# Moving the w_down sums to GpSimd's transfer queue, and placing weight rows and kept results two products earlier, in a one-core decoder layer

## Chip, core and metric

One core of a Trainium2 chip runs the whole layer as one launch. The metric is device time in microseconds, the median of several runs. The engines are named as the profile names them: PE (TensorE matmul) with its weight loads PEld, DVE (VectorE), ACT (ScalarE), POOL (GpSimd) and SP (SyncE). In this kernel SP computes nothing: it starts nearly all transfers, one after the other, and when one of them has to wait for a buffer or a result, all that stand behind it in SP's queue wait too.

## What is computed

The reference is one decoder layer on 2048 tokens of width 1024: sliding-window attention beside a convolution group, an output projection with a residual, and a SwiGLU feed-forward part with a residual. The change concerns the last of these alone:

```
hn = rms_norm(h, ffn_pre_g)
ff = (jax.nn.silu(hn @ w_gate) * (hn @ w_up)) @ w_down
h = h + rms_norm(ff, ffn_post_g)
```

D_MODEL is 1024, D_FF is 2816, and everything is float32.

## The kernel before

**Products.** A float32 matmul is made of three matmuls on 128 x 512 operands, from a rounded part and a remainder (`hl`, `w` and other tags hold the two side by side). ACT makes the rounded part of a weight (`split_f`, L824) and DVE the remainder (`lo`, L828). One *product* here is four 128-row blocks times three, that is 12 matmuls into one PSUM bank (`product`, L908).

**Feed-forward part.** The 2048 tokens are taken as two sets: tiles 0 and 1 first, then tiles 2 and 3. For each set the gate and up matrices (22 items: 11 pairs of blocks, gate and up in turn) go through the seven-product form of a 2 x 2 block multiplication. First `stage_pre` (L916) makes two of the block products for most items and stores the first of them in `keeps`. Then `stage_p1` (L992), the seven-product part, does the rest: five products for an item whose first product is kept (20 of 22 items in the first set), seven for the others, 114 products in the first set. Last, `stage_p2` (L1150) multiplies by w_down, again in seven-product form; it reads the results of p1 from `mids` and four sums of w_down blocks from `td`.

**Inside p1.** For item m, `loads(m)` (L1001) brings the two weight rows: `raw` (L1006) and `chl` (L1008), 512 KB each. `sums(m)` (L1011) has DVE make four weight sums S1 to S4 in further `chl` buffers. `fetch(m)` (L1034) brings the kept product into a `gb` buffer; ACT copies it into a PSUM bank (L1066) before the item's first product, so that the matmuls add to it. Each step first splits the weight operand of the product three steps ahead (`AHEAD = 3`), then issues its own product. Results leave through `y5` (L1076, a `gb` buffer) and `x2` (L1079, an `at` buffer), DVE adds, ACT's silu, and stores to `mids` (L1094, L1100, L1103). The pools have two buffers each for `gb`, `at` and `raw`, five for `chl`, four for `fa`, one pair for `wx` and three for `fc`.

**The w_down sums.** `stage_tsums` (L1112) runs beside the first set's p1. For each of 11 pairs it loads four w_down blocks of 256 KB (L1119: two into `wx`, two into `fc`), makes four differences on DVE in place, and stores each to `td` (L1125). One pair of `wx` buffers means that a pair's first load must wait until the previous pair's stores have landed. Beside this, DVE runs convolution taps of a later stage (tile `fc@C`).

**What sets the order.** The stages are generators. A `Lane` (L1307) hands out steps of a side stage in proportion to a cost that the main stage yields; the sums have the lane `lt` with rate `RT` (L1362), and each step's yield is its price. Code order gives priorities only. The framework then orders each engine's instructions by a simulated timeline, so a step that is ready early can be moved far ahead of its place in the code, and each engine and queue then executes its list strictly in order.

Of the kernel before, what the change touches and what calls it, by code (L numbers as in the profile page):

```python
# [26 lines left out]
T = 512  # L27
# [10 lines left out]
def layer_kernel(ctx, tc, x, xT, cols, rows, sinks, relb, onehot, w_in, w_pw, w_out, w_gate, w_up, w_down, out):  # L38
    nc = tc.nc
# [15 lines left out]
    def t_(tag, shape, dt=F32):  # L55
        return sb.tile(list(shape), dt, tag=tag, name=nm(tag), bufs=BUFS[tag])

    def f4(tag, shape=(P, D)):
        return t_(tag, shape)

    def f2(tag, shape=(P, T)):
        return t_(tag, shape)

    def hl(tag):
        return t_(tag, (P, 2, T), F32R)
# [757 lines left out]
    def split_f(x, w):  # L823
        act(w[:, 0], x, AF.Copy)  # L824
        return w

    def lo(x, w, on_pool):
        (ptt if on_pool else vtt)(w[:, 1], x, w[:, 0].bitcast(F32), ALU.subtract)  # L828
# [79 lines left out]
    def product(o, w, op, first):  # L908
        n = 0
        for k in range(4):  # L910
            ks = slice(k * P, (k + 1) * P)
            for a, b in ((0, 0), (0, 1), (1, 0)):
                mat(o, w[:, a, ks], op[k][:, b], start=first and n == 0, stop=n == 11, skip_group_check=not first)
                n += 1
# [77 lines left out]
    def stage_p1(ws, ops, mid, keep):  # L992
        PRE = PRES[ws[0]]
        L = f"F{ws[0]}"
        raws = {}
        todo = []
        for m in range(len(MATS)):
            st = [1, 2, 4, 5, 6] if m < PRE else list(range(7))
            todo += [(m, j, i, len(st)) for j, i in enumerate(st)]

        def loads(m):  # L1001
            if m < len(MATS):
                lab[0] = L
                src, pr = MATS[m]
                r0 = t_("raw", (P, 2, T))
                nc.sync.dma_start(r0, src[2 * pr].rearrange("p (a b) -> p a b", a=2))  # L1006
                r1 = t_("chl", (P, 2, T))
                nc.sync.dma_start(r1, src[2 * pr + 1].rearrange("p (a b) -> p a b", a=2))  # L1008
                raws[m] = dict(A11=r0[:, 0], A12=r0[:, 1], A21=r1[:, 0], A22=r1[:, 1])

        def sums(m):  # L1011
            if m < len(MATS):
                lab[0] = L
                r = raws[m]
                s12 = t_("chl", (P, 2, T))
                r["S1"], r["S2"] = s12[:, 0], s12[:, 1]
                vtt(r["S1"], r["A21"], r["A22"], ALU.add)
                vtt(r["S2"], r["S1"], r["A11"], ALU.subtract)
                s34 = t_("chl", (P, 2, T))
                r["S3"], r["S4"] = s34[:, 0], s34[:, 1]  # L1020
                vtt(r["S3"], r["A11"], r["A21"], ALU.subtract)
                vtt(r["S4"], r["A12"], r["S2"], ALU.subtract)

        wops = {}
        kept = {}

        def split(q):
            if q < len(todo):
                m, j, i, n = todo[q]
                lab[0] = L  # L1030
                wops[q] = split_f(raws[m][STEPS[i][1]], hl("w"))
                lo(raws[m][STEPS[i][1]], wops[q], ws[0] and i in POOL_LO)

        def fetch(m):  # L1034
            if m < PRE:
                lab[0] = L
                kept[m] = f2("gb")
                nc.sync.dma_start(kept[m], keep[m])

        loads(0)  # L1040
        sums(0)
        for q in range(AHEAD):
            split(q)
        loads(1)
        fetch(0)
        sg = {}
        for q, (m, j, i, nst) in enumerate(todo):
            pre = m < PRE
            gate = MATS[m][0] is w_gate
            pr = MATS[m][1]  # L1050
            split(q + AHEAD)
            lab[0] = L
            which, an, bn = STEPS[i]
            if len(ops.get(bn, ())) < 4:
                lh.until(f"S{ws[0]}")
                lab[0] = L
            if j == 0:
                bk = {}
                if not gate:
                    blocks = {}  # L1060
                    if pre:
                        blocks[3] = f2("fa")
                        nc.sync.dma_start(blocks[3], mid[0, pr])
                if pre:
                    bk["B"] = mm()
                    act(bk["B"], kept.pop(m), AF.Copy)  # L1066
            first = which not in bk
            if first:
                bk[which] = mm()
            o = bk[which]  # L1070
            product(o, wops.pop(q), ops[bn], first)
            if i == 0:
                bk["B"] = mm()
                act(bk["B"], o, AF.Copy)
            elif i == 1:
                y5 = f2("gb")  # L1076
                act(y5, o, AF.Copy)
            elif i == 2:
                x2 = f2("at")  # L1079
                act(x2, o, AF.Copy)  # L1080
            else:
                v = {4: y5, 5: x2}.get(i, o)
                if v is not o:
                    vtt(v, v, o, ALU.add)
                if gate:
                    s = f2("fa")
                    act(s, v, AF.Silu)
                    sg[i] = s
                else:
                    s = sg.pop(i)  # L1090
                    vtt(s, s, v, ALU.mult)
                    blocks[i] = s
                    if i in (3, 4, 6):
                        nc.sync.dma_start(mid[{3: 0, 4: 4, 6: 1}[i], pr], s)  # L1094
                    if i == 5:
                        a11, a22, a21 = blocks[3], blocks[4], s
                        for to, o_, p_, op, q_ in ((5, a22, a21, ALU.add, a22), (3, a21, a11, ALU.subtract, a21),
                                                   (2, a11, a22, ALU.subtract, a11)):
                            (ptt if ws[0] else vtt)(o_, p_, q_, op)
                            nc.sync.dma_start(mid[to, pr], o_)  # L1100
                    if i == 6:
                        (ptt if ws[0] else vtt)(s, s, blocks[3], ALU.subtract)
                        nc.sync.dma_start(mid[6, pr], s)  # L1103
            if j == nst - 4:
                sums(m + 1)
            if j == nst - 2:
                fetch(m + 1)
            if j == nst - 1:
                loads(m + 2)
            yield 2.76  # L1110

    def stage_tsums(td):  # L1112
        L = "G0"
        for pr in range(NF // 2):
            lab[0] = L
            wx = f4("wx", (P, 2, T))
            b = [wx[:, 0], wx[:, 1], f2("fc"), f2("fc")]
            for i, (f, n) in enumerate(((0, 0), (0, 1), (1, 0), (1, 1))):
                nc.sync.dma_start(b[i], w_down[2 * pr + f, :, n * T : (n + 1) * T])  # L1119
            yield 3  # L1120
            b11, b12, b21, b22 = b
            for to, o, p_, q_ in ((0, b11, b12, b11), (2, b12, b22, b12), (1, b22, b22, b11), (3, b21, b21, b22)):
                lab[0] = L
                vtt(o, p_, q_, ALU.subtract)
                nc.sync.dma_start(td[to, pr], o)  # L1125
                yield 1

    def finish(L, gb, jobs, pool=True):
        lab[0] = L
# [229 lines left out]
    YL, YL2 = 12, 20  # L1359
    YZ = 1.0  # L1360
    W_LEAD = 4.0
    RT = 0.3  # L1362
    RP = 0.1
    NS = 12
    TIE = 5
# [10 lines left out]
    lh = Lane(1.2, 0)  # L1376
    lt = Lane(RT, 0)
    lu = Lane(0.6, 0)
# [67 lines left out]
    td = dr.tile([4, NF // 2, P, T], F32, name="td")  # L1446
# [7 lines left out]
    lh.add("S0", stage_h_sums(ws, ops), lambda: f"P0.{PRE_S0}" in started and "B3" in lb.done)  # L1454
    run(stage_pre(ws, ops, mids[0], keeps[0], Q0))
    lt.add("TS", stage_tsums(td))
    run(stage_p1(ws, ops, mids[0], keeps[0]))
    lt.until("TS")
    lc.until("T2")
# [11 lines left out]
    run(stage_pre(ws, ops, mids[1], keeps[1]))  # L1471
    lf.until("E0.3")
    run(stage_p1(ws, ops, mids[1], keeps[1]))
    run(stage_p2(ws, mids[1], td, True))

# [62 lines left out]
```

## Time and profile before

| what | value |
|---|---|
| median of 3 runs | 1996.32 us (1993.41 to 1996.72) |
| the profiled execution's own time | 1994.08 us |
| its span, first to last instruction | 1992.1 us |
| mean granted TensorE clock | 0.987 |
| busy: PE, DVE, ACT, POOL | 97%, 74%, 48%, 12% of the span |
| first set's p1, by its matmuls | about 682 us to 1021 us of the span |

PE is busy nearly all of the span, so the gaps that remain lie in few places, and averages over the span hide them. Tables by stretch of the span show them: busy time of each engine, instructions that began there (x), the granted clock, and the share of the 16 DMA engines. Tables of waits tell which event ended an idle stretch; a table for SP tells what held its queue. In names, `chl@F` is a buffer of tag `chl` in stage F (gate and up), `@G` is the w_down part with its sums, `@C` the convolution, and `a<-b` is written from read. L94 is the helper that issues every DVE arithmetic instruction and L85 the one of every matmul, so groups there are told apart by tile names.

### The profile page before, as it was taken

The numbers are of one execution on the slowest core, as the hardware profiler recorded it, in microseconds if no ns is written. First come the engines' busy times: TensorE is split into PE (matmuls) and PEld (weight loads), VectorE is DVE, ScalarE is ACT, GpSimd is POOL, SyncE is SP. The second block draws the span as 40 slices with busy tenths as digits, with TensorE's granted clock in tenths as the row PEclk, the third lists the DMA queues.
The fourth block names the chain that finished last, engine by engine and source line by source line (L and its number), as shares of the span: only waits on it lengthen the run. The fifth ranks groups of instructions, "written<-read, shape, count | busy, mean of one in ns | idle before, by whom it ended". The sixth has DMA issues, their size and how long they took to land.

```text
span 1992.1 us, 26622 instructions
## 1 busy us (share of the span) xinstructions
PE 1936.4 (97%) x8730; PEld 1550.4 (78%) x8730; DVE 1467.2 (74%) x2648; ACT 953.5 (48%) x1878; POOL 247.2 (12%) x339
## 2 busy tenths in 40 slices
PE   8999999999998999899999999998899999999997
PEld 6877777777776878678888788886788888888886
DVE  4999969995875899777659964667766765455557
ACT  5455354447546533234355464656543433345443
POOL 4011111101121000000000110000023332311003
PEclk9999999999999999999999999999999999999999
DMA  8786657566659767865478787759845542466664
GB/s 307 252 305 218 210 187 257 182 214 216 225 199 322 258 222 254 280 231 190 143 238 273 255 270 243 253 201 376 289 147 170 169 159 85 142 227 197 211 195 143
DMA packets 224810, 444.06 MB, mean 223 GB/s; under 512 B 22136, under 2 KB 47904, under 8 KB 224672
## 3 DMA queue, kind: packets, MB, share of 16 engines
q1 hardware_dynamic: 212768, 429.79, 64.8%
q10 hardware_dynamic: 11904, 12.59, 1.8%
q8 instruction: 68, 1.11, 0.2%
q14 instruction: 70, 0.57, 0.1%
HBM read 327.46 MB, written 114.83 MB: 222 GB/s over the span
## 4 chain that ended last, share of the span: by engine, by line
PE 77%; DMA 11%; DVE 6%; issue 2%; ACT 2%; POOL 1%; SPq 1%; DVEq 0%; POOLq 0%; ACTq 0%
PE mm@F L85 29%; PE mm@G L85 18%; PE mm@A L85 14%; PE mm@W L85 5%; PE tr@B L85 4%; PE tr@W L85 3%; DMA gb@F<-keeps 1%; DMA chl@F<-w_gate 1%; DMA raw@F<-w_gate 1%; PE mm@U L85 1%; DMA chl@G<-h_scr 1%; DVE fc@C L94 1%; DVE w@F L94 1%; DMA td<-fc@G 1%; PE tr@B L492 1%
## 5 line engine op out<-in xcount | busy, mean ns | idle before, releaser
L94 DVE SCALAR_TENSOR_TENSOR fc@C<-glu@C,colt,fc@C 128x512 f32<-128x512 f32 x480 | 357.1, 758 | 2.8
L85 PE MATMUL mm@F<-hl@H,w@F 128*128 128x512 f32 x1056 | 256.8, 394 | 8.1 <-ACT mm@F L954 8.1
L85 PEld LDWEIGHTS mm@F<-hl@H,w@F 128*128 128x128 f32 x1056 | 200.4, 190 | 51.5 <-ACT mm@F L954 9.5
L85 PE MATMUL mm@G<-hl@G,hl@G 128*128 128x512 f32 x924 | 228.0, 392 | 1.8 <-DVE hl@G L94 1.6
L85 PE MATMUL mm@A<-hl@A,w@A 128*128 128x512 f32 x840 | 209.4, 397 | 4.4 <-ACT w@A L127 1.8
L85 PEld LDWEIGHTS mm@G<-hl@G,hl@G 128*128 128x128 f32 x924 | 171.7, 188 | 38.9 <-DVE hl@G L94 2.4
L824 ACT ACTIVATE w@F<-chl@F 128x512 fp32r<-128x512 f32 x220 | 134.8, 624 | 138.9 <-PE mm@F L85 131.4
L85 PE MATMUL mm@G<-w@G,hl@G 128*128 128x512 f32 x876 | 199.4, 389 | 0.0
L85 PEld LDWEIGHTS mm@G<-w@G,hl@G 128*128 128x128 f32 x876 | 164.4, 188 | 34.1
L85 PEld LDWEIGHTS mm@A<-hl@A,w@A 128*128 128x128 f32 x840 | 156.6, 189 | 43.1 <-issue 3.1
L94 DVE TENSOR_TENSOR w@F<-chl@F,w@F 128x512 fp32r<-128x512 f32 x198 | 145.6, 739 | 37.9 <-ACT w@F L824 37.3
L85 PE MATMUL mm@F<-mid@H,w@F 128*128 128x512 f32 x528 | 137.4, 408 | 12.5 <-ACT mm@F L954 10.6
L85 PE MATMUL mm@F<-ql@H,w@F 128*128 128x512 f32 x528 | 128.5, 391 | 6.8 <-ACT mm@F L1066 4.8
L85 PE MATMUL mm@F<-p@H,w@F 128*128 128x512 f32 x528 | 132.5, 397 | 0.0
L85 PEld LDWEIGHTS mm@F<-mid@H,w@F 128*128 128x128 f32 x528 | 103.7, 198 | 36.8 <-ACT mm@F L954 11.9
L85 PE MATMUL mm@F<-x@H,w@F 128*128 128x512 f32 x528 | 126.7, 391 | 0.0
L85 PEld LDWEIGHTS mm@F<-ql@H,w@F 128*128 128x128 f32 x528 | 98.9, 188 | 29.3 <-ACT mm@F L1066 6.2
L85 PEld LDWEIGHTS mm@F<-p@H,w@F 128*128 128x128 f32 x528 | 101.7, 193 | 21.8 <-ACT at@F L1080 0.2
L85 PEld LDWEIGHTS mm@F<-x@H,w@F 128*128 128x128 f32 x528 | 98.4, 188 | 21.1 <-issue 0.8
L127 ACT ACTIVATE w@A<-raw@A 128x512 fp32r<-128x512 f32 x110 | 67.5, 626 | 92.3 <-PE mm@A L85 63.5
L94 DVE TENSOR_TENSOR w@G<-raw@G,w@G 128x512 fp32r<-128x512 f32 x73 | 52.1, 714 | 68.8 <-ACT w@G L824 67.7
L495 POOL TENSOR_SCALAR_AFFINE_SELECT p@B<-p@B 128x512 f32<-128x512 f32 x62 | 52.9, 863 | 361.2 <-ACT p@B L493 359.8
(302 smaller groups left out, 3224.8 us busy)
## 6 DMA issues: line engine op xcount, KB each, us to landing
mids<-fa@F SPq DMA_DIRECT2D x154, 256.0 KB, 2.6
raw@A<-w_in SPq DMA_DIRECT2D x55, 512.0 KB, 4.5
w@A<-lo_in SPq DMA_DIRECT2D x84, 256.0 KB, 3.5
fc@G<-mids SPq DMA_DIRECT2D x77, 256.0 KB, 3.5
fa@G<-mids SPq DMA_DIRECT2D x75, 256.0 KB, 4.2
gb@F<-keeps SPq DMA_DIRECT2D x72, 256.0 KB, 4.5
w@W<-fold SPq DMA_DIRECT2D x32, 512.0 KB, 5.3
chl@F<-w_gate SPq DMA_DIRECT2D x22, 512.0 KB, 4.0
```

The lines of the kernel that those rows point to most:

```text
L85: r = nc.tensor.matmul(*args, **kw)
L94: r = op(*args, **kw)
L127: act(w[:, 0], raw, AF.Copy)
L492: nc.tensor.transpose(o[:, i * P : (i + 1) * P], pr[:, 4 * g + i], ident)
L495: nc.gpsimd.affine_select(out=pg[:, kb].rearrange("p (i q) -> p i q", q=P), in_=pg[:, 1].rearrange("p (i q) -> p i q", q=P), compare_op=AL ...
L824: act(w[:, 0], x, AF.Copy)
```

## The change

```diff
 (stage_p1)
             elif i == 1:
-                y5 = f2("gb")
+                y5 = f2("at")
...
             if j == nst - 4:
+                fetch(m + 1)
                 sums(m + 1)
-            if j == nst - 2:
-                fetch(m + 1)
-            if j == nst - 1:
+            if j == nst - 3:
                 loads(m + 2)
             yield 2.76
 (stage_tsums)
-                nc.sync.dma_start(b[i], w_down[2 * pr + f, :, n * T : (n + 1) * T])
-            yield 3
+                nc.gpsimd.dma_start(b[i], w_down[2 * pr + f, :, n * T : (n + 1) * T])
+            yield 2.5
...
                 vtt(o, p_, q_, ALU.subtract)
-                nc.sync.dma_start(td[to, pr], o)
-                yield 1
+                nc.gpsimd.dma_start(td[to, pr], o)
+                yield 0.6
...
-    RT = 0.3
+    RT = 0.2
```

It does five things. The kept product of the next item is fetched two products earlier. The weight rows of the item after next are loaded two products earlier. The result `y5` takes its buffer from `at` instead of `gb`, so that `gb` holds kept products alone. All 88 transfers of the w_down sums (44 loads, 44 stores) go from SP's queue to GpSimd's. A pair of the sums costs 4.9 in place of 7 and is paid at rate 0.2 in place of 0.3, so it takes 24.5 us of the main stage's count instead of 23.3 us. No arithmetic is added or removed, and no byte more or less is moved. The code lines after the edit stand one line higher (L1118 and L1124 for the sums' transfers).

SP's queue near the start of the first set's p1, before (rows `td<-` are stores of finished sums, `<-w_down` their loads, `gb<-keeps` a kept product, `raw` and `chl` weight rows, `mids` results):

```order
L1125 DMA td<-fc@G_1124_6655 128x512
L1119 DMA wx@G_1131_6712<-w_down 128x512
L1125 DMA td<-fc@G_1123_6654 128x512
L986 DMA mids_4716<-fa@F_1107_6587 128x512
L1119 DMA wx@G_1131_6712<-w_down 128x512
L1119 DMA fc@G_1132_6713<-w_down 128x512
L1038 DMA gb@F_1136_6737<-keeps_4719 128x512
L1119 DMA fc@G_1133_6714<-w_down 128x512
L1125 DMA td<-wx@G_1131_6712 128x512
L1006 DMA raw@F_1174_7002<-w_gate 128x1024
L1125 DMA td<-wx@G_1131_6712 128x512
L1008 DMA chl@F_1155_6885<-w_up 128x1024
```

The same place in the changed kernel, from the store of `mids` onward:

```order
L986 DMA mids_4716<-fa@F_1107_6587 128x512
L1006 DMA raw@F_1170_6963<-w_gate 128x1024
L1008 DMA chl@F_1153_6841<-w_up 128x1024
L1038 DMA gb@F_1185_7059<-keeps_4719 128x512
L1063 DMA fa@F_1142_6770<-mids_4716 128x512
L1006 DMA raw@F_1192_7092<-w_up 128x1024
L1038 DMA gb@F_1202_7177<-keeps_4719 128x512
L1008 DMA chl@F_1171_6965<-w_gate 128x1024
```

The rows of the sums are gone from SP's queue, and weight rows and kept products now stand next to each other; a kept product stands about one item further ahead than before.

GpSimd's queue in the changed kernel, two pairs of the sums in the middle of that part:

```order
L1118 DMA wx@G_1188_7067<-w_down 128x512 x2
L1124 DMA td<-fc@G_1155_6846 128x512
L1124 DMA td<-wx@G_1188_7067 128x512
L1118 DMA fc@G_1189_7068<-w_down 128x512
L1118 DMA fc@G_1190_7069<-w_down 128x512
L1124 DMA td<-wx@G_1188_7067 128x512
L1124 DMA td<-fc@G_1190_7069 128x512
L1124 DMA td<-fc@G_1189_7068 128x512
L1118 DMA wx@G_1218_7274<-w_down 128x512 x2
L1118 DMA fc@G_1219_7275<-w_down 128x512
```

Before, none of these rows stood on GpSimd, which has no other work in this part of either kernel. A load of the next pair now stands behind the stores of the pair before it, and behind nothing else.

## The prediction, made before the result was known

> **What bounds the kernel now.** I read the table by stretches first. Its columns are the stretch, then busy time and instructions (x) of PE, PEld, DVE, ACT and POOL, the granted clock, the DMA share and GB/s.
>
> ```profile
> 680.00:880.00 200.00, 186.33 (x779) 150.35 (x778) 169.78 (x274) 67.97 (x123) 0.00 (x0) 0.96 0.75 253
> 880.00:1010.00 130.00, 130.00 (x577) 107.61 (x576) 94.91 (x149) 53.76 (x95) 0.00 (x0) 1.00 0.52 167
> 780.00:880.00 100.00, 88.52 (x359) 70.59 (x358) 79.28 (x128) 31.45 (x57) 0.00 (x0) 0.93 0.82 279
> 1410.00:1770.00 360.00, 360.00 (x1592) 298.05 (x1591) 223.96 (x299) 148.05 (x265) 97.17 (x68) 1.00 0.48 160
> ```
>
> The first set's seven-product part (p1) falls in two. From 880 us on PE is full at clock 1.00: 577 matmuls in 130 us, 0.2253 us each, so 2.70 us for a product of 12. Before that, 200 us hold 779 where 888 would fit: 109 are missing, which is **24.5 us lost**, most of it between 780 and 880. The second set's p1 loses nothing (360.00 of 360). The w_down sums run in the first part only (the last load into `wx` starts at 863.9 us, in a row further down), so the loss lies where they run. The waits say what PE stood for (680 to 1010 us), and then what DVE, ACT and SP stood for from 680 to 880:
>
> ```profile
> PE mm@F L85 <- DVE gb@F L94: 5.0, 3, 2.2
> PE mm@F L85 <- ACT mm@F L1066: 4.8, 2, 4.5
> PE mm@F L85 <- ACT w@F L824: 1.9, 1, 1.9
> PE mm@F L85 <- ACT fa@F L1087: 1.0, 1, 1.0
> PE mm@F L85 <- DVE fa@F L94: 0.9, 1, 0.9
> ```
>
> ```profile
> DVE chl@F L94 <- DMA chl@F<-w_gate: 7.7, 5, 2.7
> DVE chl@F L94 <- DMA chl@F<-w_up: 7.4, 4, 4.1
> DVE wx@G L94 <- issue: 4.8, 3, 2.3
> DVE wx@G L94 <- DMA fc@G<-w_down: 4.5, 4, 1.8
> DVE wx@G L94 <- DMA wx@G<-w_down: 3.9, 2, 2.7
> DVE fa@F L94 <- DMA mids<-fa@F: 0.9, 1, 0.9
> DVE w@F L94 <- ACT w@F L824: 0.6, 1, 0.6
> ACT mm@F L1066 <- DMA gb@F<-keeps: 55.9, 11, 11.7
> SPq L1125 <- DVE wx@G L94: 21.4, 16, 4.3
> SPq L1119 <- DMA td<-fc@G: 21.0, 9, 4.7
> SPq L1119 <- DMA td<-wx@G: 15.8, 8, 4.2
> SPq L1125 <- DVE fc@G L94: 10.7, 17, 1.6
> ```
>
> PE waits for ACT and DVE; ACT waits 55.9 us for kept products; DVE waits 15.1 us for weight rows and 13.2 us for blocks of w_down. The last two DVE rows add 1.5 us, and 169.8 us busy plus these waits make the 200. All these transfers stand in SP's queue, and SP spends 68.9 us of the 200 waiting on behalf of the sums. The chain of waits shows the queue at work:
>
> ```profile
> 795.74 7.20 DMA chl@F<-w_gate
> ...
> 820.02 5.69 DMA td<-fc@G
> 825.72 2.90 DMA fc@G<-w_down
> 829.37 2.48 DMA td<-wx@G
> ...
> 832.79 5.75 DMA chl@F<-w_gate
> ...
> 867.37 6.68 DMA gb@F<-keeps
> 874.13 0.61 ACT mm@F L1066
> ```
>
> A weight row starts at 832.79 only after a store, a load and a store of the sums before it, and the copy of a kept product at 874.13 ends the loss. Of the 24.5 us, the table of PE's waits names 13.6 in all; I put the rest to the granted clock, 0.93 to 0.96 here against 1.00.
>
> **The change part by part.** *DVE's budget.* DVE has 274 instructions in 169.78 us, 0.62 us each. Counted in the orders, 267 DVE instructions lie between the second and the last of the sums beside 63 products before, and 285 beside 69 now. Before: 267 x 0.62 = 165.5 us of work against 63 x 2.70 = 170.3 us of PE, a slack of 4.8; DVE's idle 30.2 us less this slack is 25.4, so the 24.5 us are explained by DVE's waits. Now: 177 against 186.6 us, a slack of 9.9, because the sums stretch over six more products. What DVE still waits beyond 9.9 us is lost.
>
> *Waits removed.* With no rows of the sums in SP's queue, weight rows and kept products start when their buffers are free. For kept products two `gb` buffers now serve nothing else, and the fetch stands an item further ahead (13 us or more, against a landing of 4.5 us below), so I count ACT's wait for them as 0. For weight rows I leave 3 us of 15.1, since without the sums there is still some:
>
> ```profile
> DVE chl@F L94 <- DMA chl@F<-w_up: 3.4, 3, 1.8
> DVE chl@F L94 <- DMA chl@F<-w_gate: 2.1, 3, 0.8
> ```
>
> These are from 880 to 1010 us, where DVE is ahead and may wait. What is late next is the sums themselves.
>
> *The sums in GpSimd's queue.* The trace has no transfer started by GpSimd. Rows for the same transfers on SP, with issue time in ns (min/median/max), and landing times as medians and as min/median/max, then a GpSimd instruction of the same tile size:
>
> ```profile
> L1119 SPq DMA_DIRECT2D wx@G<-w_down x22: 332/403/1540, 424.0 to 863.9; - x22
> DMA to landing us min/median/max: 2.8/4.0/7.1
> chl@F<-w_gate SPq DMA_DIRECT2D x22, 512.0 KB, 4.0
> gb@F<-keeps SPq DMA_DIRECT2D x72, 256.0 KB, 4.5
> L828 POOL TENSOR_TENSOR w@F<-chl@F,w@F 128x512 fp32r<-128x512 f32 x22 | 31.6, 1438 | 307.8 <-ACT w@F L824 264.4 <-DVE gb@F L94 33.2 <-DVE at@F L94 10.2
> ```
>
> Between the last difference of one pair and the first of the next, GpSimd issues about one store and two loads. At 0.40 us each they cost what they cost on SP; at 1.44 us, the dearest near row, 3 x 1.04 = 3.1 us more per pair. The order gives them 10.7 DVE rows of room on average, against 7.9 before: 2.8 x 0.62 = 1.7 us. So ten pairs wait 13.2 + 10 x (0 - 1.7), that is nothing, up to 13.2 + 10 x (3.1 - 1.7) = 27 us. I take 18, on the dearer side because two loads more must follow before the second difference. The sum: 18 + 3 + 1.5 = 22.5 us of waits, less 9.9 of slack, leaves 12.6 lost; 24.5 - 12.6 = **11.9 us gained**.
>
> Behind a waiting transfer on GpSimd stand only transfers of the sums (POOL is at 0.00 in both stretches). Only the first pair's early load and store stand beside attention, where GpSimd idles (the bracket is the idle time before the row):
>
> ```profile
> 438.62 2.85 POOL L495 TENSOR_SCALAR_AFFINE_SELECT p@B<-p@B 128x512 f32<-128x512 f32 x4 [31.42 <-ACT p@B L493]
> ```
>
> I take 0, and at most 3 if its difference comes late on DVE. Stores of `mids` move past nothing that waits.
>
> *Free edits.* `y5` in `at`: after p1, the first `at@G` load waits for a buffer that is freed later in the last item than before; PE is full to the end of the 880 to 1010 row, with matmuls of the next tile's projection at hand behind it, so 0, at most 3. In the second set PE is full, its weight rows only come earlier, so 0, at most 2 either way.
>
> A rule of the Trainium skill speaks against the new queue. DVE's only copy-like instruction from 680 to 880 is this:
>
> ```profile
> L94 DVE TENSOR_SCALAR fc@C<-glu@C,colt 128x512 f32<-128x512 f32 x1 | 0.5, 544 | 0.0
> ```
>
> The Trainium skill, page "SBUF — State Buffer", sections "SBUF: two separate sides" and "Who interferes with whom", says that GpSimd cannot write a transfer's descriptors while DVE runs in a two-port fast mode, which copies and tensor-scalar operations can enter, and advises SP or ACT for starting such transfers. By that rule and this row one transfer is held for half a microsecond, and the sum stays; a stretch full of such operations would decide otherwise.
>
> **Rivals.** *Sums later than I count.* If each of ten pairs waits 4 us instead of 1.8, DVE waits 40 + 4.5, of which 34.6 are lost, 10.1 more than now: 2004. At 2.8 us the waits are 32.5, the loss 22.6, and 1992 comes out. For it speaks DVE's small slack, against it the wider spacing. Centre: 1993.
>
> *The shared engines, not the queue.* The stretch from 780 to 880 moves 279 GB/s at a DMA share of 0.82. If weight rows land in 6 to 7 us because the engines are loaded, starting them elsewhere changes nothing: 1994. Against it: SP's 68.9 us, and the landing medians near 4. The Trainium skill, page "DMA: Bandwidth & Descriptors", section "Issuing engines are not separate DMA queues", states this rule: starting transfers from several engines saves only the issue time.
>
> *Slower: GpSimd holds DVE.* In the second set DVE's instructions take 223.96 / 299 = 0.75 us beside 68 GpSimd instructions, 0.13 more than the 0.62 of the first: 39 us, or 0.57 us for each. If a transfer started there did the same, 85 of them would add 48 us to a DVE with no slack left: 1982 + 48 = 2030, and at half the price 2006. Above 0.14 us per transfer (11.9 / 85) the gain is gone. Against it: those 68 read two tiles each.
>
> **How the numbers follow.** Against the profiled execution's 1994.08 us the sum gives 1982.2; that execution lies between the lowest run shown (1993.41) and the median (1996.32), so I carry the sum over as 1982.5. Case by case: the forecast 0.62, from 1969.6 (DVE's waits all within its slack) to 1988 (2.4 us per pair); later sums 0.19, of which 0.09 still faster, 0.07 the same and 0.03 slower; shared engines 0.06, of which 0.05 the same and 0.01 faster; GpSimd holding DVE 0.13, all slower. Faster means by over 0.2% (4 us, about what a measurement of this kernel tells from no change): 0.62 + 0.09 + 0.01 = 0.72. The same: 0.07 + 0.05 = 0.12. Slower: 0.03 + 0.13 = 0.16. The range, 1969 to 2005, holds the first three cases and leaves out most of the last.
>
> **What would show it.** Right: matmuls between 680 and 880 us rise from 779 to 830 or more; ACT's wait for `keeps` there falls below 10 us; DVE's wait for `chl` rows below 5; DVE's wait for `wx@G` stays between 10 and 27 us. Wrong: DVE's mean above 0.65 us per instruction in that stretch; the landing of weight rows unchanged; gaps at 1000 to 1030 us or in the second set's p1.

## The result, and the profile after

The changed kernel takes **1984.38 us** (median of 8 runs, 1978.81 to 1988.28) against 1996.34 us (8 runs, 1993.41 to 1999.60): a ratio of 0.9939, 95% interval 0.9924 to 0.9953, or 12.0 us faster. The profiled execution is the slowest of the eight (1988.28 us, span 1986.6 us, mean clock 0.989), so its losses are a little above the typical ones.

The table by stretches (stretch, then busy time and instructions of PE, PEld, DVE, ACT and POOL, granted clock, DMA share, GB/s), after:

```profile
680.00:880.00 200.00, 190.56 (x824) 154.96 (x823) 175.69 (x285) 75.42 (x133) 43.09 (x80) 0.99 0.76 255
880.00:1010.00 130.00, 130.00 (x571) 107.60 (x570) 93.62 (x149) 51.56 (x91) 1.62 (x3) 0.99 0.53 174
1410.00:1770.00 360.00, 360.00 (x1590) 298.18 (x1589) 223.70 (x291) 144.30 (x255) 97.69 (x68) 1.00 0.47 161
```

PE began 824 matmuls between 680 and 880 us, 45 more than before. At 0.2253 us each that is 10.1 us; 64 are still missing (888 - 824), or **14.4 us**. In this pair of executions not all of the 10.1 us is kept. Just ahead of the stretch the changed one began 11 matmuls fewer at a lower clock (first the kernel before, then the changed one):

```profile
580.00:680.00 100.00, 91.12 (x398) 72.71 (x397) 73.46 (x111) 62.80 (x110) 10.87 (x26) 0.97 0.88 293
580.00:680.00 100.00, 91.43 (x387) 72.73 (x386) 70.08 (x106) 61.01 (x107) 12.55 (x28) 0.93 0.88 291
```

From 880 to 1010 us it began 6 fewer, and the two spans differ by only 5.5 us (1992.1 and 1986.6). The two stretches in which PE was full are still full. DVE takes 175.69 / 285 = 0.616 us per instruction, as before, while GpSimd starts transfers beside it.

What PE, DVE and SP waited for in the same 200 us, after (engine, line, releaser; us in total, times, longest):

```profile
PE mm@F L85 <- DVE at@F L94: 5.0, 3, 2.3
PE mm@F L85 <- DVE fa@F L94: 3.4, 2, 2.3
PE mm@F L85 <- ACT at@F L1077: 0.6, 1, 0.6
PE mm@F L85 <- DVE w@F L94: 0.5, 1, 0.5
```

```profile
DVE chl@F L94 <- DMA chl@F<-w_gate: 6.9, 3, 3.5
DVE wx@G L94 <- DMA fc@G<-w_down: 5.7, 3, 3.3
DVE wx@G L94 <- issue: 3.1, 3, 2.5
DVE wx@G L94 <- DMA wx@G<-w_down: 2.9, 2, 1.6
DVE chl@F L94 <- DMA chl@F<-w_up: 2.5, 1, 2.5
```

```profile
SPq L1100 <- DVE fa@F L94: 40.8, 16, 9.0
SPq L1006 <- DVE chl@F L94: 32.9, 12, 6.4
SPq L1094 <- DVE fa@F L94: 26.1, 11, 8.5
SPq L1008 <- DVE w@F L94: 19.2, 13, 3.5
```

Before, ACT's first row was 55.9 us for `gb<-keeps`; after, ACT has no such row in this stretch. DVE waits 9.4 us for the weight rows in `chl` (15.1 before; another 0.9 us for `raw` is not shown) and 11.7 us for the sums (13.2). PE's rows name 9.5 us, nearly all of it for results of DVE. SP no longer stands for the sums: it stands for the results that it stores (L1094, L1100) and for buffers of weight rows to come free (L1006, L1008).

The stalls that SP had are on GpSimd now. Two rows of its waits, and one of its timeline (start, us, engine, line, operation, and in brackets the idle time before):

```profile
POOL td L1124 <- DVE wx@G L94: 99.6, 18, 33.5
POOL fc@G L1118 <- DMA y_scr<-fc@C: 34.5, 1, 34.5
```

```profile
760.81 0.54 POOL L1118 DMA_DIRECT2D fc@G<-w_down  x1 [34.55 <-DMA y_scr<-fc@C]
```

Nobody else stands behind them there. One wait inside the stretch is long: a load needs one of the three `fc` buffers and waits 34.5 us, until the convolution taps that were accumulated in it have been stored (`y_scr<-fc@C`). The sums stop for that time and are bunched behind it. The new queue did not bring this: before, two loads into `fc` on SP's queue start at 729.66 and 766.00 us, the second just after such a store has landed (765.98 us). The other long wait, 33.5 us, is that of the first store of the stretch, for a difference that DVE makes at 685.6 us.

### The profile page after: what moved, and what is told of

The parts are those of the page before. It is cut to its first block, busy times and chain, and to the rows that moved or that the text cites. A ratio compares the mean times of both kernels' runs of the same rounds, so it can differ in the third digit from the quotient of the medians.

```text
span 1986.6 us, 26668 instructions
## 1 busy us (share of the span) xinstructions
PE 1933.8 (97%) x8730; PEld 1549.4 (78%) x8730; DVE 1469.8 (74%) x2648; ACT 957.8 (48%) x1878; POOL 292.4 (15%) x427
## 4 chain that ended last, share of the span: by engine, by line
PE 75%; DMA 10%; DVE 9%; issue 3%; ACT 2%; POOL 1%; SPq 0%; DVEq 0%; POOLq 0%; ACTq 0%
PE mm@F L85 30%; PE mm@G L85 16%; PE mm@A L85 14%; PE mm@W L85 5%; PE tr@B L85 4%; DVE fc@C L94 3%; PE tr@W L85 2%; DMA raw@F<-w_gate 1%; PE mm@U L85 1%; DMA chl@G<-h_scr 1%; DMA gb@F<-keeps 1%; DMA td<-wx@G 1%; DVE w@F L94 1%; DMA raw@F<-w_up 1%; DMA raw@A<-w_in 1%
## 5 line engine op out<-in xcount | busy, mean ns | idle before, releaser
L94 DVE TENSOR_TENSOR w@F<-chl@F,w@F 128x512 fp32r<-128x512 f32 x198 | 147.4, 747 | 32.9 <-ACT w@F L824 32.5
L85 PEld LDWEIGHTS mm@F<-p@H,w@F 128*128 128x128 f32 x528 | 99.2, 188 | 20.6
```

Source lines behind the costliest of these rows:

```text
L85: r = nc.tensor.matmul(*args, **kw)
L94: r = op(*args, **kw)
```

## The experiments

Ratios are to the kernel before, timed on the same chip beside the kernels in question. There it had a median of 1996.00 us over 24 runs (beside `e1`, `e7`, `n2` and `n6`), 1996.43 over 29 (beside `e8`, `q_act`, `n1` and `m_rc2`) and 1994.69 over 9 (beside `s2` and `e4`). For each kernel I show the row of the stretch 680 to 880 us, in which 888 matmuls would fit. A row is one execution, and the rows of two kernels with the same lists of instructions differ by 15 matmuls (824 here, 839 in `s2_queue_y5`), so a difference of that size between rows says little; the ratios decide. The theory: the gain has two parts, the queue and `y5`'s buffer. The main rivals: one of them carries all of it, or the earlier `fetch` and `loads` do.

**The queue alone** (`e1_queue_only`), before with:

```diff
-                nc.sync.dma_start(b[i], w_down[2 * pr + f, :, n * T : (n + 1) * T])
+                nc.gpsimd.dma_start(b[i], w_down[2 * pr + f, :, n * T : (n + 1) * T])
...
-                nc.sync.dma_start(td[to, pr], o)
+                nc.gpsimd.dma_start(td[to, pr], o)
```

> Only the queue of the sums' 88 transfers changes; y5 stays in gb, fetch, loads and rates stay. Theory A (DVE's waits, caused by SP's queue and by the shared gb buffers, set the loss): about two thirds of the gain, 6 to 10 us faster than before; DVE's wait for weight rows (15.1 us from 680 to 880) falls to 10 or less, ACT's wait for kept products (55.9 us) stays above 20 because gb still holds y5. Theory B (only the kept products mattered, freed by the second gb buffer): 0 to 3 us faster. Theory C (the queue does all): 11 to 13 us faster, ACT's wait for kept products gone.

Measured: 1991.90 us (12 runs), ratio 0.9981 (0.9967 to 0.9994), 3.8 us faster.

```profile
680.00:880.00 200.00, 187.84 (x797) 151.38 (x796) 171.41 (x278) 69.20 (x124) 42.02 (x78) 0.97 0.72 245
```

```profile
ACT mm@F L1066 <- DMA gb@F<-keeps: 39.0, 11, 8.7
```

797 matmuls, 18 more than before. With every row of the sums gone from SP's queue, ACT still waits 39.0 of 55.9 us for kept products. So the queue was the lesser part of that wait, and the queue alone is a third of the gain. This wait and DVE's for weight rows, 9.8 us, are where theory A had them; the gain is between theory A's 6 to 10 us and theory B's 0 to 3.

**The buffer alone** (`e7_y5_only`), before with:

```diff
-                y5 = f2("gb")
+                y5 = f2("at")
```

> Only y5 moves from gb to at; all transfers stay on SP. In the printed order PE's list is the same as with fetch and loads moved too, so this stands for the whole part about earlier loads. Theory A: 3 to 6 us faster than before, ACT's wait for kept products falls below 30 us, DVE's wait for weight rows stays above 10 us. Theory B: 10 to 13 us faster. Theory C: within 2 us of before.

Measured: 1987.27 us (9 runs), ratio 0.9961 (0.9946 to 0.9976), 7.8 us faster by the ratio.

```profile
680.00:880.00 200.00, 189.38 (x815) 153.93 (x814) 174.37 (x283) 74.52 (x131) 0.00 (x0) 0.98 0.78 260
```

```profile
SPq L1125 <- DVE wx@G L94: 16.2, 16, 2.9
SPq L1119 <- DMA td<-fc@G: 15.6, 12, 3.7
SPq L1119 <- DMA td<-wx@G: 14.5, 7, 3.9
SPq L1125 <- DVE fc@G L94: 13.6, 17, 2.0
PE mm@F L85 <- DVE at@F L94: 7.8, 5, 3.8
PE mm@F L85 <- DVE fa@F L94: 2.7, 1, 2.7
```

One word brings twice what 88 moved transfers bring: ACT's row for `keeps` is gone, and PE has 815 matmuls, although SP still waits 59.9 us for the sums (68.9 before). The gain is again between two ranges, theory A's 3 to 6 us and theory B's 10 to 13, and the split that I expected, more for the queue than for the buffer, was the wrong way round. PE's rows show where the gain comes in: before, PE waited 7.7 us for ACT (three rows), with the queue alone 9.3 us, and here it waits for DVE alone. I read it so that an ACT copy waiting for a kept product holds up the weight splits and copies behind it, and PE with them. The tag also changes the built order (DVE's list differs from the one before at 448 of its 2648 places), and no run parts the buffer from the order that follows from it.

**Both, without the rest** (`s2_queue_y5`), after with the other three edits taken back:

```diff
-                fetch(m + 1)
                 sums(m + 1)
-            if j == nst - 3:
+            if j == nst - 2:
+                fetch(m + 1)
+            if j == nst - 1:
                 loads(m + 2)
...
-            yield 2.5
+            yield 3
...
-                yield 0.6
+                yield 1
...
-    RT = 0.2
+    RT = 0.3
```

> The changed kernel with only two of its five edits: the sums' transfers in GpSimd's queue and y5 in at. Fetch and loads stand where they stood before, and the prices and the rate of the sums are those of before. Theory (only these two edits act, because the lists of instructions of all engines come out the same as in the changed kernel): the time of the changed kernel within noise, ratio to before 0.992 to 0.996, about 1984, and 815 to 830 matmuls between 680 and 880 us. Rival (the earlier fetch and loads bring some of the gain): 3 to 6 us slower than that, a ratio above 0.9965. Against the kernel of the same call with the sums still on SP: 2 to 6 us faster if the queue still has its worth of 3.8 us once y5 is out of gb; the same within 1.5 us if the freed gb buffers have already taken the queue's gain.

**All but the queue** (`e4_all_but_queue`), after with `nc.sync` in place of `nc.gpsimd` in the two lines of the first diff:

> The changed kernel with the sums' 88 transfers put back into SP's queue; y5 in at, the earlier fetch and loads, the prices and the rate stay. Theory (gains add: y5 some 8 us, queue some 4): the time of the kernel with y5 alone in at, ratio 0.995 to 0.9975, about 1988, with 810 to 820 matmuls between 680 and 880 us; ACT waits for keeps under 5 us there. Rival 1 (the queue does nothing more once y5 is out of gb): the same time as the other kernel of this call within 1.5 us. Rival 2 (earlier fetch and loads are worth something even on SP): ratio below 0.9945.

Measured: 1982.91 us (5 runs), ratio 0.9941 (0.9927 to 0.9954), and 1985.30 us (5 runs), ratio 0.9952 (0.9939 to 0.9964). First `s2_queue_y5`, then `e4_all_but_queue`:

```profile
680.00:880.00 200.00, 194.27 (x839) 157.44 (x838) 176.40 (x287) 75.58 (x133) 43.58 (x81) 0.99 0.76 259
```

```profile
680.00:880.00 200.00, 188.51 (x810) 153.56 (x809) 172.72 (x281) 71.65 (x125) 0.00 (x0) 0.98 0.77 258
```

Two edits of five give the whole gain: 0.9941 against 0.9939. The built programs tell why: row by row, every engine's list of instructions is the same in `s2_queue_y5` as in the changed kernel. So beside these two edits a call that stands two products earlier in the code moves nothing, and neither does the new rate; presumably the framework already starts a fetch or a load as early as its buffer allows. With the sums on SP the other three edits do move rows (SP's list differs between `e4_all_but_queue` and `e7_y5_only` at 85 of 1334 places), but the two ratios, 0.9952 and 0.9961, are not told apart. In the execution of `s2_queue_y5` the stretch carries the whole gain: it has 60 matmuls more than before, 13.5 us, and the span, 1979.1 us, is 13.0 us shorter. Beside `y5`'s edit the queue is worth about 2.4 us (5 runs against 5, whose ranges overlap), 3.8 us by itself; with the 7.8 us of the buffer the two parts add up nearly.

**Which buffer** (`e8_kept_at`), after with the tags exchanged: `y5` alone in `gb`, and kept products in `at`, which `x2` uses too:

```diff
-                kept[m] = f2("gb")
+                kept[m] = f2("at")
...
-                y5 = f2("at")
+                y5 = f2("gb")
```

> The changed kernel with the two tags swapped: kept products share at with x2, and y5 has gb alone. Theory K (the gain of the y5 edit is that kept products get two buffers of their own, so that the next one is on its way before the present one is read): like the queue alone, 1989 to 1994, with ACT's wait for kept products from 680 to 880 us above 25 us. Theory Y (what counted was that y5 no longer held a gb buffer long, whoever shares with the kept products): like the changed kernel, 1981 to 1987, and that wait below 10 us.

Measured: 1995.55 us (12 runs), ratio 0.9985 (0.9971 to 0.9999).

```profile
680.00:880.00 200.00, 186.13 (x791) 150.90 (x790) 166.12 (x269) 69.45 (x126) 38.36 (x71) 0.97 0.71 235
```

```profile
ACT mm@F L1066 <- DMA at@F<-keeps: 35.5, 10, 6.3
```

Kept products and `y5` are apart in this kernel too, so parting them isn't what counts. What counts is that kept products have two buffers to themselves: sharing with `x2` in place of `y5` brings ACT's wait back (35.5 us), and most of the gain goes, with the queue as free as in the changed kernel. The wait is as theory K had it; the time is a little above its 1989 to 1994 us.

**Any other queue?** (`q_act`), after with the sums' transfers started by ACT (`nc.scalar` in the two lines):

> The changed kernel with the sums' 88 transfers started by ACT instead of GpSimd. If it only matters that they leave SP's queue: within 3 us of the changed kernel. If it matters that the queue that takes them has nothing else to do: stores that wait for a difference hold ACT's weight splits and copies behind them, 5 to 25 us slower than the changed kernel, 1990 to 2010.

Measured: 1994.16 us (12 runs), ratio 0.9992 (0.9975 to 1.0009).

```profile
680.00:880.00 200.00, 185.68 (x786) 149.23 (x785) 166.27 (x269) 68.88 (x122) 0.00 (x0) 0.97 0.74 245
```

```profile
ACT w@F L824 <- DVE wx@G L94: 16.1, 7, 4.0
...
ACT w@F L824 <- DVE fc@G L94: 9.3, 3, 5.6
ACT w@F L824 <- DMA td<-wx@G: 7.0, 1, 7.0
...
ACT at@F L1077 <- DMA td<-fc@G: 6.4, 1, 6.4
```

SP is as free of the sums as in the changed kernel, yet even `y5`'s gain is lost: a store that waits for DVE's difference now holds ACT's next weight split. The four rows are 38.8 us of ACT standing still for the sums. ACT issues such a transfer in less time than GpSimd does (the loads of `wx`: min/median/max in ns, first and last start), first `q_act`, then the changed kernel:

```profile
L1118 ACTq DMA_DIRECT2D wx@G<-w_down x22: 339/396/486, 423.6 to 872.2; - x22
```

```profile
L1118 POOL DMA_DIRECT2D wx@G<-w_down x22: 541/541/762, 424.9 to 872.2; - x22
```

The Trainium skill, page "DMA: Bandwidth & Descriptors", section "Issuing engines are not separate DMA queues", says that starting transfers on another engine saves only the time of starting them. By that sentence ACT should have done as well as GpSimd; the ratios, 0.9992 and 0.9939, and ACT's four rows say that what is saved or lost here is the waiting in front of a transfer, not its start.

**The differences left out** (`n1_no_diff`), after without the 44 differences; the blocks of w_down are stored to `td` as they were loaded:

```diff
-                vtt(o, p_, q_, ALU.subtract)
```

> The changed kernel without the 44 differences on DVE: the w_down blocks go to td as they were loaded, so that part of the computation is left out and the transfers stay. Theory A (what the changed kernel still loses is DVE's time and DVE's waits for w_down blocks): 27 us of DVE's work and 11.7 us of its waits are gone, matmuls from 680 to 880 rise from 824 to 870 or more, 1971 to 1976. Rival (the loss is set by late weight rows and the DMA engines): 1980 to 1986, matmuls below 845, DVE's wait for weight rows stays near 9 us.

Measured: 1979.73 us (6 runs), ratio 0.9907 (0.9888 to 0.9925).

```profile
680.00:880.00 200.00, 198.72 (x868) 163.35 (x867) 164.62 (x264) 81.14 (x144) 19.07 (x35) 0.99 0.65 218
```

868 of 888: of the 14.4 us that are left in the changed kernel's row, 9.9 are gone without the sums' work on DVE and its waits, or 6.5 us against the 839 of `s2_queue_y5`. The ratios differ by 0.0032, or 6.4 us, and the medians by 4.7. So a part of the rest is the differences, but both expectations missed: the matmuls came near theory A's 870, and the time stayed above its 1971 to 1976 us. The order also changes ahead of the stretch (2708 matmuls before 580 us, 2746 in the changed kernel), so this is not the price of the differences alone. DVE still waits 13.3 us for weight rows here, in two rows as above, and little is lost by it: it is ahead, and also waits 11.7 us for PE.

**The differences on GpSimd** (`n2_pool_diff`), after with:

```diff
-                vtt(o, p_, q_, ALU.subtract)
+                ptt(o, p_, q_, ALU.subtract)
```

> The changed kernel with the 44 differences of w_down blocks made by GpSimd instead of DVE. Theory A (DVE's budget is what is left): 44 x 0.62 = 27 us leave DVE's list, and if each GpSimd difference holds DVE 0.57 us as in the second set, 25 us come back, but its waits for w_down blocks (11.7 us) go altogether; so 8 to 14 us faster than the changed kernel, 1971 to 1976. Rival (what is left is not DVE but the DMA engines, share 0.80 from 780 to 880): within 3 us of the changed kernel. Rival (GpSimd with two inputs holds DVE for its whole 1.44 us): 10 us or more slower than the changed kernel.

Measured: 2005.53 us (6 runs), ratio 1.0054 (1.0037 to 1.0071).

```profile
680.00:880.00 200.00, 182.32 (x772) 147.27 (x771) 177.95 (x234) 70.72 (x126) 83.55 (x98) 0.97 0.68 232
```

Fewer instructions on DVE, and more busy time: 0.76 us each. Three groups of DVE in this stretch (count, busy us, mean ns), first here, then in the changed kernel:

```profile
L94 DVE TENSOR_TENSOR chl@F<-raw@F,chl@F 128x512 f32<-128x512 f32 x27 | 25.4, 969 | 0.1
L94 DVE TENSOR_TENSOR fa@F<-fa@F,fa@F 128x512 f32<-128x512 f32 x20 | 19.3, 964 | 3.5 <-DMA mids<-fa@F 3.4
L94 DVE TENSOR_TENSOR at@F<-at@F,mm@F 128x512 f32<-128x512 f32 x24 | 15.9, 677 | 0.9 <-PE mm@F L85 0.8
```

```profile
L94 DVE TENSOR_TENSOR chl@F<-raw@F,chl@F 128x512 f32<-128x512 f32 x28 | 18.7, 684 | 0.0
L94 DVE TENSOR_TENSOR at@F<-at@F,mm@F 128x512 f32<-128x512 f32 x26 | 17.5, 679 | 0.2 <-PE mm@F L85 0.2
L94 DVE TENSOR_TENSOR fa@F<-fa@F,fa@F 128x512 f32<-128x512 f32 x24 | 16.4, 682 | 1.2 <-DMA mids<-fa@F 1.2
```

The two additions of two SBUF tiles take 0.28 us more (`w@F`, the largest group, 0.842 us against 0.683); the one whose second operand is a PSUM bank (`mm`) takes no more. Over the stretch that is (0.76 - 0.616) x 234 = 34 us for 33 differences begun on GpSimd (POOL groups of 9, 8, 8 and 8), 1.0 us of DVE for each, more than the 0.62 us that DVE saves. The time, 21 us above the changed kernel's, is the last rival's, its price of 1.44 us is not. The Trainium skill, page "SBUF — State Buffer", section "Who interferes with whom", has this: a DVE instruction with two SBUF inputs contends with a GpSimd instruction that reads SBUF, and one with at most one such input, outside the two-port fast modes, does not. The rows agree.

**The taps' accumulator apart** (`n6_own_tap`), after with one of the three `fc` buffers kept for the taps, so that no load waits 34.5 us:

```diff
-    BUFS = dict(x=4, p=4, wx=1, gb=2, hl=8, ql=4, chl=5, mid=4, mb=2, fa=4, at=2, fc=3, glu=2, yt=1, raw=2, w=6)
+    BUFS = dict(x=4, p=4, wx=1, gb=2, hl=8, ql=4, chl=5, mid=4, mb=2, fa=4, at=2, fc=2, fy=1, glu=2, yt=1, raw=2, w=6)
...
-        y = f2("fc")
+        y = f2("fy")
...
-                rawa[i] = f2("fc" if last else "at" if i < 2 else "fa")
+                rawa[i] = f2(("fy" if i % 3 == 2 else "fc") if last else "at" if i < 2 else "fa")
```

> The changed kernel with an own buffer for the convolution's accumulator (fc has two buffers then), so that no w_down load waits for it (one did for 34.5 us) and the pairs of sums follow each other evenly from the start, but end at product 61 instead of 73. Theory A by the budget: 278 DVE instructions x 0.62 = 172 us stand against 61 products x 2.70 = 165 us, so there is no slack, and all of DVE's waits count: 5 to 15 us slower than the changed kernel, 1990 to 2000. Rival (the loss is the bunching of eight pairs after that wait): 5 to 10 us faster than the changed kernel.

Measured: 1986.29 us (10 runs), ratio 0.9953 (0.9937 to 0.9969).

```profile
680.00:880.00 200.00, 187.95 (x813) 150.75 (x812) 177.36 (x288) 73.74 (x129) 41.47 (x77) 1.00 0.76 261
```

Neither expectation: no better and no clearly worse than the changed kernel. The sums are evenly spaced now and DVE waits 7.3 us for them instead of 11.7, but they end beside product 61 instead of 73, so the same work has fewer products to hide beside. These two may offset each other, so what the bunching costs by itself is not shown.

**Taps at half the rate** (`m_rc2`), after with RC2 at 0.2 in place of 0.4, so that DVE has fewer taps beside the sums:

> The changed kernel with the convolution taps beside this part at half their rate (RC2 0.2 instead of 0.4): in the printed order the sums now end beside product 79 instead of 73, and the taps are spread evenly (6 to 10 in ten products instead of 11 to 14 first and 3 to 5 later). Theory A: DVE's list is no shorter but more even, so a part of the rest comes back, 1977 to 1983. Rival (evenness does not matter, waits do): within 3 us of the changed kernel. Slower if taps that are left over fall on the next part, where DVE has 70% to do.

Measured: 1997.24 us (12 runs), ratio 1.0002 (0.9989 to 1.0015). Two stretches of this kernel, then the second of them in the changed kernel:

```profile
680.00:880.00 200.00, 188.88 (x806) 153.47 (x806) 167.14 (x269) 72.93 (x130) 31.87 (x59) 0.97 0.71 236
...
1010.00:1330.00 320.00, 312.89 (x1409) 256.22 (x1408) 229.88 (x375) 160.54 (x280) 21.75 (x48) 0.99 0.70 236
```

```profile
1010.00:1330.00 320.00, 318.08 (x1443) 261.53 (x1442) 227.45 (x370) 171.13 (x296) 15.71 (x48) 1.00 0.74 250
```

The taps come back later, as the last expectation had it: between 1010 and 1330 us DVE runs 110 of them against 81 in the changed kernel (`fc@C`, SCALAR_TENSOR_TENSOR), 34 matmuls or 7.7 us are missing there, and nothing is gained in the stretch of the sums, where DVE waits 18.0 us for weight rows instead.

No kernel that does the whole work was clearly faster than the changed one.

## Why the prediction was right, and where its working was not

The forecast, 11.9 us faster and 1982.5 us, met 12.0 us and 1984.38. Step by step:

- **Where the gain lies: right.** In the slowest execution the stretch has 824 matmuls against a forecast of 830 or more, 10.1 us more work than before, of which the span keeps 5.5; in `s2_queue_y5`, whose instructions are the same, it has 839, and the span keeps all of it. In the slowest execution 14.4 us stay lost where 12.6 were forecast.
- **ACT's wait for kept products: right in the size, without a price.** I counted it as 0 after, and it is gone. But the sum was made of DVE's waits alone, so this wait's end was given no worth, and `y5`'s edit stood under "Free edits". It is the larger part: 7.8 us by itself. This is the step that failed in the working. I read the 55.9 us as one more sign of SP's full queue; the queue alone leaves 39.0 of it, and two buffers of its own remove it with the queue as full as before.
- **What the earlier fetch does: wrong.** "The fetch stands an item further ahead" is seen in the order, but the freed buffer does that. Beside the other two edits, the earlier calls move no instruction.
- **The weight rows: too low.** 3 us were forecast, with a limit of 5 as the sign of being right; 9.4 came (and 12.1 in `s2_queue_y5`'s trace, 7.0 and 5.1). The term took the wait to come from the sums' rows in SP's queue. But the queue alone leaves 9.8 us, the buffer alone, with the sums still on SP, 10.8, and both together no clearly smaller wait. Where SP stood for the sums before, it now stands 32.9 us for a buffer of weight rows (L1006).
- **The sums' waits: too high.** 18 us were forecast, 11.7 came. Three issues of 0.54 us cost 0.4 us more per pair than on SP, not the 3.1 us of the dear end. But with 0.4 the prediction's own formula gives 13.2 + 10 x (0.4 - 1.7) = 0.2 us, so the wider room did not save what the formula takes off either; 11.7 lies between two wrong terms.
- **The small waits: too low.** 1.5 us were forecast, 3.9 came (four rows, the 0.9 us for `raw` among them).
- **The slack of 9.9 us: about right.** DVE's idle time in the changed kernel is 200 - 175.69 = 24.3 us, of which 14.4 are lost: 9.9. That it fits to the tenth is chance: in `s2_queue_y5`, with the same lists, 23.6 us are idle and 11.0 lost (49 matmuls), which leaves 12.6. The queue's edit brings it: in the built programs the 69 products stand beside the sums with the queue alone too, 65 with the buffer alone. The budget is less exact where the sums stay on SP: for `e7_y5_only` it has 275 x 0.62 = 170.5 against 65 x 2.70 = 175.5 us, a slack of 5.0, and idle time of 25.6 us; 20.6 us should be lost, and 888 - 815 = 73 matmuls, or 16.4 us, are. What covers the other 4 us stays open.
- **The clock: not shown.** I put the 10.9 of 24.5 us that PE's waits don't name to the granted clock. In `n6_own_tap` the clock of the stretch is 1.00, PE is idle for 12.0 us, and yet 75 matmuls or 16.9 us are missing: 4.9 us are lost there to neither. What takes them stays open.

So the two large errors on DVE's waits, 6.4 too low and 6.3 too high, cancelled by luck, and the right sum has the wrong causes in it: it gave SP's queue nearly everything.

**The rivals.** *Shared engines:* refuted as the whole story by 0.9939, though the landing of weight rows has hardly moved. Medians over the whole span of the changed kernel (`chl@F<-w_gate` took 4.0 us before):

```profile
chl@F<-w_gate SPq DMA_DIRECT2D x22, 512.0 KB, 4.3
...
wx@G<-w_down POOLq DMA_DIRECT2D x22, 256.0 KB, 3.6
td<-wx@G POOLq DMA_DIRECT2D x22, 256.0 KB, 4.0
```

A row in "What would show it" took an unchanged landing as a sign against me; it isn't one, since a wait can shrink (15.1 to 9.4 us) while the landing stays. *GpSimd holding DVE:* not for transfers (0.616 us per DVE instruction with 80 GpSimd instructions in the stretch), while for two-input arithmetic `n2_pool_diff` ends at 2005.53 us, the lower edge of that rival. The price that I took from the second set belongs to arithmetic and did not carry over to transfers; for arithmetic it was too low here, 0.57 us each against 1.0. *Later sums:* the sums' waits did not grow (11.7 us, 13.2 before), and the long stop of 34.5 us has its like in the kernel before.

## What to carry to other kernels

When an engine waits for a load, ask first whether the load's buffer is free and only then whether its queue is: undo one at a time, since a full queue and a shared buffer make the same row in a table of waits. A queue that starts transfers waits in order, so transfers that must wait for results belong on an engine that has nothing else to do in that stretch; on busy ACT they cost here all that both edits had saved. And where a framework orders instructions by when their buffers come free, moving a call in the code may move nothing: compare the built order before counting on it.

## What the runs showed of the hardware

- A transfer of 128 x 512 float32 started by GpSimd takes 0.54 us of its time, against 0.40 us on SP and on ACT (medians for `wx`, in the changed kernel, the kernel before and `q_act`), and lands in 3.5 to 5.1 us (medians of four kinds), 3.5 to 4.5 us on SP. DVE is not slowed by it: 0.616 us per instruction beside 80 GpSimd instructions, 0.62 us before.
- Arithmetic on GpSimd with two SBUF tiles takes 1.3 to 1.7 us for 128 x 512 and lengthens DVE's own two-tile additions from 0.68 to 0.97 us in the two groups shown, those with a PSUM operand not at all (`n2_pool_diff`).
